# A hybrid RWKV-7 / S5 layer on one core: late tiles two abreast, a gate pair in the other order, stores on another queue, products on another engine, one scan behind the level

## The chip, the cores and the metric

The kernel runs on one core of a Trainium2 chip. The metric is the device time in microseconds of one launch. The engines of the core are named as in the profile: PE is TensorE (matrix products; PEld its weight loads), DVE is VectorE, ACT is ScalarE, POOL is GpSimd and SP is SyncE, which issues most of the DMA transfers. An engine whose name ends in q (SPq, POOLq) is its queue of DMA issues.

## What is computed

One layer over 1024 tokens of width 1024, in fp32:

```python
h = rms_norm(x, norm_mix_pre)
proj = h @ w_in                         # RWKV r, k, v, low-rank downs | S5 input u | two gates
gates = sigmoid(proj[..., -2048:] + b_gate)
o_rwkv = rwkv7_branch(...) @ w_branch_rwkv   # per head: S = S*w + (S a) b' + v k',  y = S r
o_s5 = s5_branch(...) @ w_branch_s5          # complex diagonal scan, then gelu(y) * sigmoid(y @ w_glu + b_glu)
mixed = (g_rwkv * o_rwkv + g_s5 * o_s5) @ w_out
x = x + rms_norm(mixed, norm_mix_post)
h = rms_norm(x, norm_ffn_pre)
z = causal_conv3(h @ w_up); gate, val = split(z)
x = x + rms_norm((gelu(gate) * val) @ w_down, norm_ffn_post)
```

## The kernel before, in words

All activations stand transposed: channels on the 128 partitions, tokens along the free dimension, in two halves of 512 tokens (`th` 0 and 1). A product of fp32 accuracy is made of three matmuls: both operands are split into a high and a low part (weights `wh` on ACT at L157 and `wl` on DVE at L158, from a tile `wf` that SP loads at L156), and `mm3_steps` issues for each of the contraction tiles high by high (L173), low by high (L174) and high by low (L175). One output tile of 128 channels by 512 tokens over eight contraction tiles is therefore 24 matmuls.

PE's instruction order is written out by hand. `drive` steps through generators ("lanes"), each of which names the time until it may go on (constants T_...), in a clock that it advances itself; whenever no lane is due, the next step of a list of background tiles (`fill`) is issued. DVE, ACT, POOL and SP take their order from a scheduler with priorities; each of them then runs strictly in that order.

From 0 to about 255 us the kernel makes the S5 scan and the first projections (`s5_lane`, `tab_lane`, `mix_in`). The projection tiles are stored to memory, all on SP's queue: TZ, TA and TG by `lowrank` (L999), RKV by `rkv` (L1006), and the gates GT by `gate_tiles` (L1035), where ACT writes tanh of the tile at L1034.

From about 255 to 815 us the RWKV branch runs in four pieces i = 0 to 3 (pairs of head groups by token halves), each with two fronts (`rwkv_front`), a matrix inverse (`rwkv_inv`), a `rwkv_level` and a `rwkv_chain` of eight steps; the background is the sixteen gate tiles, two at a time for both halves, then `merge(0)` and the output projection of half 0 with the S5 GLU tiles of half 1 (`out_glu`). A front loads k, TZ, TA and r at L659 and v at L696 (SP), scans TZ (L674, DVE), and makes the products `ar1` and `bk1` on GpSimd (L683 and L684); DVE's L681 and L714 stand beside these. The level begins with two DVE transposes (L787) whose result `ld` PE multiplies at L790. `merge(0)` needs the RWKV output of half 0 (YR, loaded at L1155 on POOL's queue and split at L227/L228) and the S5 output (YU, loaded on POOL's queue at L1119, gelu on ACT, split at L1125/L1126).

From about 815 to 1045 us comes the tail: the S5 part of the merge of half 1 (`merge_s5`), the last `rwkv_out`, its RWKV part (`merge_rk`, results halved and split at L232/L233), the output projection of half 1 (`outproj`), two norms of each half (`mid_norms`) and the first MLP units (`first_units`, whose inputs `h` are split at L227/L228). The rest is the fast up-projection (to about 1400 us) and the down-projection.

## Time and profile before

| | |
|---|---|
| time, median of 3 runs | 1628.59 us (1625.99 to 1630.82) |
| time of the profiled execution | 1626.5 us |
| its span | 1624.7 us |
| mean granted TensorE clock | 0.967 |
| PE busy | 1505.0 us (93%) |
| DVE busy | 1157.2 us (71%) |
| ACT busy | 717.6 us (44%) |
| POOL busy | 175.9 us (11%) |

PE is busy for 93% of the span, and the granted clock is a little under full: a stall of PE shows both as idle time ahead of an instruction, and in the stretches after it in which the clock column is below 1. The idle times are listed by the line that waited and by the instruction that ended the wait. DMA issues are not counted as busy on the queue that issues them.

### The profile page before, as it was taken

Reading aid. Unit: us, or ns where it says so; the run is one execution under the profiler, and the core shown is the slowest. Engines: PE = TensorE matmul, PEld = TensorE weight load, DVE = VectorE, ACT = ScalarE, POOL = GpSimd, SP = SyncE. Lnnn points to the kernel's source line nnn. Section 1 sums busy time; section 2 is a strip of 40 time slices with the busy share of each in tenths; the row PEclk is TensorE's granted clock in tenths of the full one; section 3 lists DMA queues with packets and bytes.
Section 4 is the critical chain, followed back from the end, with each engine's and each line's share of the span. In section 5 each row is a group of like instructions: output and inputs, shape, how many; then the busy total and the mean of one; then the engine's idle time right before and its main releaser. Section 6 shows DMA issues by size and latency. Waiting matters only on the chain. (4 is left out here: it accounts for less than half of the span.)

```text
span 1624.7 us, 23434 instructions
## 1 busy us (share of the span) xinstructions
PE 1505.0 (93%) x8644; PEld 1200.3 (74%) x8644; DVE 1157.2 (71%) x2103; ACT 717.6 (44%) x1173; POOL 175.9 (11%) x251
## 2 busy tenths in 40 slices
PE   5998998999989997899978999999999999999995
PEld 4887887787666774666756878788888888788784
DVE  7888774565534687575478479987777777788777
ACT  5445433232444344446633445544454444443451
POOL 0030003133012133211020000000000000000000
PEclk9999999999998997999988999999999999999997
DMA  5353344343341256535255363322222224862722
GB/s 190 110 158 124 97 130 143 117 130 116 90 145 67 76 179 175 142 106 163 84 187 190 107 193 130 137 71 91 78 78 91 91 79 160 293 227 96 234 85 104
DMA packets 116387, 213.72 MB, mean 132 GB/s; under 512 B 22272, under 2 KB 28416, under 8 KB 116272
## 3 DMA queue, kind: packets, MB, share of 16 engines
q1 hardware_dynamic: 102960, 175.78, 33.8%
q0 software_dynamic: 11152, 32.20, 6.7%
q10 hardware_dynamic: 2160, 4.24, 0.7%
q8 instruction: 68, 1.11, 0.3%
q14 instruction: 47, 0.39, 0.1%
HBM read 157.12 MB, written 52.95 MB: 129 GB/s over the span
## 5 line engine op out<-in xcount | busy, mean ns | idle before, releaser
L173 PE MATMUL gm<-hh,wh 128*128 128x512 f32 x688 | 298.5, 434 | 17.9 <-DVE ev L961 5.5
L174 PE MATMUL gm<-hl,wh 128*128 128x512 f32 x688 | 277.8, 404 | 3.3 <-DVE hl L1126 2.0
L175 PE MATMUL gm<-hh,wl 128*128 128x512 f32 x688 | 276.4, 402 | 0.0
L158 DVE TENSOR_TENSOR wl<-wf,wh 128x512 fp32r<-128x512 f32 x183 | 127.9, 700 | 115.1 <-ACT wh L157 113.4
L157 ACT CAST wh<-wf 128x512 fp32r<-128x512 f32 x183 | 113.3, 620 | 185.2 <-PE gm L174 94.0
L173 PEld LDWEIGHTS gm<-hh,wh 128*128 128x128 f32 x688 | 133.5, 194 | 54.6 <-ACT hh L1125 6.3
L174 PEld LDWEIGHTS gm<-hl,wh 128*128 128x128 f32 x688 | 134.0, 195 | 30.6 <-DVE hl L228 4.3
L175 PEld LDWEIGHTS gm<-hh,wl 128*128 128x128 f32 x688 | 133.6, 194 | 30.2 <-DVE wl L158 0.7
L1608 PE MATMUL d<-xl,wh 128*128 128x512 f32 x308 | 120.3, 391 | 3.1 <-DVE xl L228 3.1
L1607 PE MATMUL d<-xh,wh 128*128 128x512 f32 x308 | 120.2, 390 | 2.0 <-DVE zg L1463 2.0
L1609 PE MATMUL d<-xh,wl 128*128 128x512 f32 x308 | 119.9, 389 | 0.0
L1433 PE MATMUL rp<-t,h 128*128 128x512 f32 x216 | 84.4, 391 | 2.2 <-ACT p L1447 1.6
L1435 PE MATMUL rp<-t,l 128*128 128x512 f32 x216 | 84.2, 390 | 0.5 <-DVE l L228 0.5
L1434 PE MATMUL rp<-t,h 128*128 128x512 f32 x216 | 84.1, 389 | 0.0
L1608 PEld LDWEIGHTS d<-xl,wh 128*128 128x128 f32 x308 | 57.8, 188 | 16.7 <-DVE xl L228 4.8
L1607 PEld LDWEIGHTS d<-xh,wh 128*128 128x128 f32 x308 | 57.8, 188 | 14.4 <-DVE zg L1463 2.4
L1609 PEld LDWEIGHTS d<-xh,wl 128*128 128x128 f32 x308 | 57.8, 188 | 11.9
L227 ACT CAST h<-r 128x1024 fp32r<-128x1024 f32 x34 | 35.8, 1054 | 61.1 <-PE rp L1434 29.6
L228 DVE TENSOR_TENSOR l<-r,h 128x1024 fp32r<-128x1024 f32 x34 | 41.6, 1225 | 29.2 <-ACT h L227 27.7
L1454 DVE SCALAR_TENSOR_TENSOR y<-zv,vecs,y 128x1023 f32<-128x1023 f32 (+1 forms) x36 | 46.1, 1281 | 8.6 <-ACT y L1452 8.6
L1433 PEld LDWEIGHTS rp<-t,h 128*128 128x128 f32 x216 | 40.5, 188 | 11.8 <-ACT p L1447 2.4
L1447 ACT COPY p<-rp 128x512 f32<-128x512 f32 x54 | 31.1, 575 | 37.2 <-PE rp L1435 37.2
(446 smaller groups left out, 3400.4 us busy)
## 6 DMA issues: line engine op xcount, KB each, us to landing
wf<-in_w_in_dram SPq DMA_DIRECT2D x72, 256.0 KB, 3.0
r<-in_w_up_dram SPq DMA_DIRECT2D x36, 512.0 KB, 3.9
st<-in_w_down_dram SPq DMA_DIRECT2D x55, 256.0 KB, 4.3
st<-ACT SPq DMA_DIRECT2D x44, 256.0 KB, 4.7
wf<-in_w_up_dram SPq DMA_DIRECT2D x36, 256.0 KB, 2.9
ACT<-y POOLq DMA_DIRECT2D x18, 512.0 KB, 2.9
GT<-ev SPq DMA_DIRECT2D x32, 256.0 KB, 2.4
wf<-in_w_br_dram SPq DMA_DIRECT2D x32, 256.0 KB, 2.8
```

Of the source, the lines that this page charges most:

```text
L157: nc.scalar.copy(h[:, :n], f[:, :n])
L158: nc.vector.tensor_tensor(l[:, :n], f[:, :n], h[:, :n].bitcast(F32), ALU.subtract)
L173: mm(ps, a, xh[k], start=k == 0, stop=False)
L174: mm(ps, a, xl[k], start=False, stop=False)
L175: mm(ps, b, xh[k], start=False, stop=k == n - 1)
L1433: mm(ps, wh[:, c], xh, start=first and k == 0, stop=False, skip_group_check=True)
L1434: mm(ps, wh[:, c], xl, start=False, stop=False, skip_group_check=True)
L1435: mm(ps, wl[:, c], xh, start=False, stop=k == 3, skip_group_check=True)
L1454: V.scalar_tensor_tensor(y[:, lag:], z[:, 0:1024 - lag], self.vec(nme, i), y[:, lag:], ALU.mult, ALU.add)
L1607: mm(ps, wh[:, c], xh[:, x], start=start, stop=False, skip_group_check=True)
L1608: mm(ps, wh[:, c], xl[:, x], start=False, stop=False, skip_group_check=True)
L1609: mm(ps, wl[:, c], xh[:, x], start=False, stop=stop, skip_group_check=True)
```

## The change

Every one of these is in one version. PE's matmuls are the same in number and shape.

1. `skewed` computes two output tiles abreast: six of the eight contraction tiles for both, then the last two for both. It is used for the first two tiles of `outproj` of half 1 and for the first MLP unit's two tiles (`up1_pair`, there in the order KORD in which `mid_norms` makes the inputs).
2. The stores of TZ, TA, TG, RKV and GT, and the loads of v, are issued by GpSimd's queue instead of SP's.
3. The scan of a front is put, for the scheduler only, behind the transposes of the level before it (`levelled`).
4. The products `ar1` and `bk1` (four for each front, 32 in all) are made on DVE instead of GpSimd.
5. The last gate pair (tiles 14 and 15) does half 1 first; between the halves `merge_values` issues the preparation of the merge's inputs, S5's (`xs0`, through `ev` tiles) included, which `merge` issued after its first gate before. YR is loaded straight into the tile of the low part.
6. The last `rwkv_out` gets the priority HPN and comes due T_LF = 11 after its start instead of T_LN = 16; the S5 GLU tiles of half 1 are issued up to two after each output tile from the fifth on (before: one, from the fourth on), with y loaded ahead of the matmuls; `mid_norms(0)` starts when `merge_rk` has been issued instead of in `merge_s5`, and T_N5 goes from 55 to 24.

The order shows the third and fourth on DVE, at the level of the second piece (i = 1), whose transposes read `gr_3231`; `ld_4601` and `ld_4610` are the TZ tiles of the next piece's two fronts. Before:

```order
L906 TENSOR_TENSOR ld_4584<-ld_4584,ld_4586 128x512
L158 TENSOR_TENSOR wl_4854<-wf_4855,wh_4853 128x512
L906 TENSOR_TENSOR ld_4584<-ld_4584,ld_4588 128x512
L674 SCALAR_TENSOR_TENSOR ld_4601<-csts,ld_4601 128x512
L787 STREAM_TRANSPOSE ld_4632<-gr_3231 32x512 x2
L674 SCALAR_TENSOR_TENSOR ld_4610<-csts,ld_4610 128x512
L681 TENSOR_TENSOR ld_4827<-ld_4827,ld_4599 128x512
L714 SCALAR_TENSOR_TENSOR ld_4605<-ld_4605,vecs,ld_4827 128x512
L681 TENSOR_TENSOR ld_4888<-ld_4888,ld_4608 128x512
L714 SCALAR_TENSOR_TENSOR ld_4614<-ld_4614,vecs,ld_4888 128x512
```

and in the changed kernel:

```order
L929 TENSOR_TENSOR ld_4584<-ld_4584,ld_4588 128x512
L801 STREAM_TRANSPOSE ld_4632<-gr_3231 32x512 x2
L686 SCALAR_TENSOR_TENSOR ld_4601<-csts,ld_4601 128x512
L686 SCALAR_TENSOR_TENSOR ld_4610<-csts,ld_4610 128x512
L695 TENSOR_TENSOR ld_4827<-ld_4827,ld_4599 128x512
L697 TENSOR_TENSOR ar_4593<-ld_4605,gr_4595 64x8x64
L697 TENSOR_TENSOR ar_4593<-ld_4614,gr_4595 64x8x64
L698 TENSOR_TENSOR bk_4594<-ld_4827,ld_4601 64x8x64
L697 TENSOR_TENSOR ar_4593<-ld_4605,gr_4595 64x8x64
L697 TENSOR_TENSOR ar_4593<-ld_4614,gr_4595 64x8x64
L728 SCALAR_TENSOR_TENSOR ld_4605<-ld_4605,vecs,ld_4827 128x512
L698 TENSOR_TENSOR bk_4594<-ld_4827,ld_4601 64x8x64
```

The transposes now stand ahead of both scans, directly behind the last sums of `rwkv_out`, and products of `ar` and `bk` follow the scans on the same engine.

The fifth shows on ACT, around the end of the gate tiles, where `hh` from L1125 (L1148 now) is the high part of an S5 input and L1034 (L1057 now) empties a gate tile. Before:

```order
L1034 ACTIVATE ev_5985<-gm_5960,hb_b_gate 128x512
L227 CAST hh_5928<-ld_5926 128x512
L157 CAST wh_6139<-wf_6141 128x512
L157 CAST wh_6167<-wf_6169 128x512
L757 COPY x_6378<-csts 128x512
L157 CAST wh_6227<-wf_6229 128x512
L1120 ACT_TABLE_LOAD
L1120 ACTIVATE ld_6039<-ld_6039 128x512
L1120 ACTIVATE ld_6046<-ld_6046 128x512
L157 CAST wh_6298<-wf_6300 128x512
L1125 CAST hh_6042<-ld_6039 128x512
L1125 CAST hh_6049<-ld_6046 128x512
```

and in the changed kernel:

```order
L1057 ACTIVATE ev_5905<-gm_5816,hb_b_gate 128x512
L239 CAST hh_5951<-hl_5952 128x512
L157 CAST wh_6014<-wf_6016 128x512
L1143 ACT_TABLE_LOAD
L1143 ACTIVATE ev_5908<-ev_5908 128x512
L157 CAST wh_6065<-wf_6067 128x512
L1148 CAST hh_5911<-ev_5908 128x512
L1143 ACTIVATE ev_5915<-ev_5915 128x512
L701 COPY gr_5702<-rsy_5862 128x512
L157 CAST wh_6088<-wf_6090 128x512
L1148 CAST hh_5918<-ev_5915 128x512
L1143 ACTIVATE ev_5922<-ev_5922 128x512
```

The gelu of the S5 inputs and their high parts stand now between the two halves of the last gate pair (two more gate tiles are emptied behind the last row shown), with the load of the activation table ahead of them; before, they came after the last gate tile and five weight casts.

The first shows on PE at the start of `outproj` of half 1, where `t` are the last four of the eight inputs, in the order in which `merge_rk` finishes them, and `mm` and `ch` the first two output tiles. Before, from the second of these four:

```order
L173 MATMUL mm_8691<-t_1676_8621,wh_8685 128x512
L174 MATMUL mm_8691<-t_1677_8622,wh_8685 128x512
L175 MATMUL mm_8691<-t_1676_8621,wl_8686 128x512
L173 MATMUL mm_8691<-t_1683_8648,wh_8685 128x512
L174 MATMUL mm_8691<-t_1684_8649,wh_8685 128x512
L175 MATMUL mm_8691<-t_1683_8648,wl_8686 128x512
L173 MATMUL mm_8691<-t_1690_8675,wh_8685 128x512
L174 MATMUL mm_8691<-t_1691_8676,wh_8685 128x512
L175 MATMUL mm_8691<-t_1690_8675,wl_8686 128x512
L173 MATMUL ch_8732<-e_8486,wh_8720 128x512
L174 MATMUL ch_8732<-e_8487,wh_8720 128x512
L175 MATMUL ch_8732<-e_8486,wl_8721 128x512
```

and in the changed kernel, from the same input:

```order
L174 MATMUL mm_8630<-t_1654_8548,wh_8612 128x512
L175 MATMUL mm_8630<-t_1655_8549,wh_8612 128x512
L176 MATMUL mm_8630<-t_1654_8548,wl_8613 128x512
L174 MATMUL ch_8631<-e_8413,wh_8618 128x512
L175 MATMUL ch_8631<-e_8414,wh_8618 128x512
L176 MATMUL ch_8631<-e_8413,wl_8619 128x512
L174 MATMUL ch_8631<-e_8440,wh_8618 128x512
L175 MATMUL ch_8631<-e_8441,wh_8618 128x512
L176 MATMUL ch_8631<-e_8440,wl_8619 128x512
L174 MATMUL ch_8631<-e_8467,wh_8618 128x512
L175 MATMUL ch_8631<-e_8468,wh_8618 128x512
L176 MATMUL ch_8631<-e_8467,wl_8619 128x512
```

The third and fourth of them (t_1683 and t_1690 before) followed at once; now the first six inputs of the second tile stand ahead of them.

The diff, without what only passes things on:

```diff
-    def mm3_steps(self, ps, w, wk, xh, xl):
+    def mm3_steps(self, ps, w, wk, xh, xl, ks=None, first=True, last=True):
         wh, wl = w
-        n = len(xh)
-        for k in range(n):
+        ks = list(ks or range(len(xh)))
+        for k in ks:
             j = wk + k
-            self.open += (k == 0) - (k == n - 1)
+            a0, z0 = first and k == ks[0], last and k == ks[-1]
+            self.open += a0 - z0
             mm = self.nc.tensor.matmul
-            mm(ps, a, xh[k], start=k == 0, stop=False)
+            mm(ps, a, xh[k], start=a0, stop=False)
             mm(ps, a, xl[k], start=False, stop=False)
-            mm(ps, b, xh[k], start=False, stop=k == n - 1)
+            mm(ps, b, xh[k], start=False, stop=z0)
+    def skewed(self, tiles, xs, ks, late):
+        xh, xl = [x[0] for x in xs], [x[1] for x in xs]
+        ps = [self.gmp() for _ in tiles]
+        ks = list(ks)
+        for p, (w, _) in zip(ps, tiles):
+            yield from self.mm3_steps(p, w, 0, xh, xl, ks[:-late], last=False)
+        for p, (w, use) in zip(ps, tiles):
+            yield from self.mm3_steps(p, w, 0, xh, xl, ks[-late:], first=False)
+            use(p)
...
-        def ld(src):
+        def ld(src, q=nc.sync):
             t = self.tg("ld", NLD)
-            nc.sync.dma_start(t, src[:, o])
+            q.dma_start(t, src[:, o])
...
-        V.tensor_tensor_scan(tz, self.cst("smask"), tz, 0.0, ALU.mult, ALU.add)
+        scan = V.tensor_tensor_scan(tz, self.cst("smask"), tz, 0.0, ALU.mult, ALU.add)
+        if self.levelled is not None:
+            self.tc.add_manual_dep(scan.ins, self.levelled.ins.name, ORDER)
...
         for h, sl in enumerate(HS):
-            G.tensor_tensor(ar1[h], c64(r)[sl], pe[sl, :, 1:65], ALU.mult)
-            G.tensor_tensor(bk1[h], c64(tk)[sl], c64(tz)[sl], ALU.mult)
+            V.tensor_tensor(ar1[h], c64(r)[sl], pe[sl, :, 1:65], ALU.mult)
+            V.tensor_tensor(bk1[h], c64(tk)[sl], c64(tz)[sl], ALU.mult)
...
             V.scalar_tensor_tensor(bk0[h], c64(kk)[sl], 0.5, c64(tz)[sl], ALU.mult, ALU.mult)
-        v = ld(self.RKV[8 + p])
+        v = ld(self.RKV[8 + p], G)
...
         for h, sl in enumerate(top):
-            V.transpose(xz[sl].rearrange("p u c t -> p (u c) t"), gr[sl, :, :, h, sl].rearrange("p u c t -> p (u c) t"))
+            self.levelled = V.transpose(xz[sl].rearrange("p u c t -> p (u c) t"), gr[sl, :, :, h, sl].rearrange("p u c t -> p (u c) t"))
...
+    def urgent(self, gen):
+        while True:
+            with self.tc.high_priority(HPN - HP2):
+                r = next(gen, None)
+            if r is None:
+                return
+            yield r
...
         V.tensor_tensor(yn, yn, y.unsqueeze(2).to_broadcast([128, 16, 64]), ALU.mult)
-        yield 0, T_LN
+        yield 0, T_LF if final else T_LN
...
         ws = [self.load_w(self.a["w_in"][mt]) for mt, _ in jobs]
-        for th in range(2):
+        for th in (1, 0) if between else (0, 1):
                 use(th, ps)
-            if between and th == 0:
+            if between and th:
...
                         nc.gpsimd.tensor_scalar(t, t, 1.0, 1.0, ALU.add, ALU.mult)
-                    nc.sync.dma_start(dst[p][:, th * 512:th * 512 + 512], t)
+                    nc.gpsimd.dma_start(dst[p][:, th * 512:th * 512 + 512], t)
                 y = self.shifted(ps, mt, th)
-                self.nc.sync.dma_start(self.RKV[mt][:, th * 512:th * 512 + 512], y)
+                self.nc.gpsimd.dma_start(self.RKV[mt][:, th * 512:th * 512 + 512], y)
...
             self.nc.scalar.activation(t, ps, AF.Tanh, bias=self.hb["b_gate"][:, m:m + 1], scale=0.5)
-            self.nc.sync.dma_start(self.GT[m][:, th * 512:th * 512 + 512], t)
+            self.nc.gpsimd.dma_start(self.GT[m][:, th * 512:th * 512 + 512], t)
...
-    def glu_tile(self, m, xs, t, y, to):
+    def glu_tile(self, m, xs, t, y, to, ahead=False):
         w = self.load_w(self.a["w_glu"][m])
+        if ahead:
+            y = lambda v=y(): v
...
+        if not self.xs0:
+            for b in range(4):
+                y = self.s5_y(self.ev((128, 8, 64)), b, 0)
+                self.xs0.append(self.pair(1, 4 + b))
+                self.s5_split(*self.xs0[b], y)
             return
-        self.br0 = []
         for k in range(4):
-            y = self.tg("ld", NLD)
-            self.nc.gpsimd.dma_start(y, self.YR[k][:, 0:512])
-            self.br0.append(self.pair(0, k))
-            self.split(*self.br0[k], y)
+            hh, hl = self.pair(1, k)
+            self.nc.gpsimd.dma_start(hl.bitcast(F32), self.YR[k][:, 0:512])
+            self.br0.append((hh, hl))
+            self.split(hh, hl, hl.bitcast(F32))
...
             self.merge_values()
-        br = self.br0
-        xs = []
-        def inputs():
-            for b in range(4):
-                y = self.s5_y(self.tg("ld", NLD, s8), b, 0)
-                xs.append(self.pair(1, 4 + b))
-                self.s5_split(*xs[b], y)
+        br, xs = self.br0, self.xs0
             if i < NK:
-                first.append(self.hp[1].tile([128, 512], F32, tag=f"h{'lh'[i // 4]}{i % 4}", name=self.nm("hl"), bufs=1))
+                first.append(self.hp[0].tile([128, 512], F32, tag=f"h{'lh'[i // 4]}{i % 4}", name=self.nm("hl"), bufs=1))
                 yield from self.gate(0, i, 0, br[0:4], self.ev(), first[i])
-            if i == 0:
-                inputs()
...
             self.br5[m] = self.slots("eb", m)
-            yield from self.glu_tile(m, xs, self.et(), lambda: self.s5_y(self.et(s8), m, 1), self.br5[m])
+            yield from self.glu_tile(m, xs, self.et(), lambda: self.s5_y(self.et(s8), m, 1), self.br5[m], True)
...
             yield from self.outproj_tile(0, m, mg, self.mx0)
-            if self.glu and m >= 3 and self.now >= self.glu_ready:
-                yield from self.glu.pop(0)
+            for _ in range(2):
+                if self.glu and m >= 4 and self.now >= self.glu_ready:
+                    yield from self.glu.pop(0)
...
             self.split_half(*mg[m], t)
+        self.merged = True
...
-        nc, hp = self.nc, self.hp[th]
         yield from self.mm3_steps(ps, w, 0, [x[0] for x in mg], [x[1] for x in mg])
+        self.outproj_end(th, m, mx, ps)
+    def outproj_end(self, th, m, mx, ps):
+        nc, hp = self.nc, self.hp[th]
...
     def outproj(self, th, mg, mx):
-        for m in range(NK):
+        yield from self.skewed([(self.load_w(self.a["w_out"][m]), lambda ps, m=m: self.outproj_end(th, m, mx, ps))
+                                for m in range(2)], mg, range(NK), 2)
+        for m in range(2, NK):
...
         else:
-            yield 0, lambda: self.y0 is not None
-            yield 0, T_RS
+            yield 0, lambda: self.merged
+            yield 0, T_PN
...
         self.h[th] = [None] * NK
-        for k in (0, 4, 1, 5, 2, 6, 3, 7):
+        for k in KORD:
...
+    def up1_pair(self, i, th):
+        y = []
+        yield from self.skewed([(self.load_w(self.a["w_up"][j]), lambda ps, j=j: y.append(self.conv1(ps, j, th)))
+                                for j in (i, FT + i)], self.h[th], KORD, 2)
+        return y
...
         for i in range(NFIRST):
-            ga = yield from self.up1_steps(i, th)
-            va = yield from self.up1_steps(FT + i, th)
+            if i:
+                ga = yield from self.up1_steps(i, th)
+                va = yield from self.up1_steps(FT + i, th)
+            else:
+                ga, va = yield from self.up1_pair(i, th)
...
         self.mark, self.chained, self.glu, self.glu_ready = False, False, [], 0.0
-        self.opened, self.outs, self.br0, self.y0 = False, 0, None, None
+        self.opened, self.outs, self.br0, self.xs0, self.y0, self.merged, self.levelled = False, 0, [], [], None, False, None
...
             out = self.rwkv_out(d)
-            r = next(out)
-            if i == 3:
-                yield r
-                yield from out
+            if i < 3:
+                r = next(out)
+            else:
+                yield from self.urgent(out)
 NEVA = 4
-T_KN, T_BK, T_GR, T_INV, T_LV, T_CH, T_LN = 17.0, 13.0, 2.5, 62.0, 1.0, 0.8, 16.0
+T_KN, T_BK, T_GR, T_INV, T_LV, T_CH, T_LN, T_LF = 17.0, 13.0, 2.5, 62.0, 1.0, 0.8, 16.0, 11.0
 T_X, T_GLU = 3.0, 25.0
-T_N0, T_RS, T_N1, T_N2, T_N4, T_N5, T_N3 = 2.5, 4.0, 2.2, 5.0, 1.6, 55.0, 2.0
+T_N0, T_RS, T_N1, T_N2, T_N4, T_N5, T_N3 = 2.5, 4.0, 2.2, 5.0, 1.6, 24.0, 2.0
 NET = 5
+T_PN = 8.0
+KORD = (0, 4, 1, 5, 2, 6, 3, 7)
...
 HPW, HPN = 400000, 500000
+ORDER = mybir.DependencyInfo(mybir.DependencyClass.NoSync, mybir.DependencyReason.SCHED_ONLY)
```

## The prediction

> **What bounds the kernel now.** I read the page first, then PE's waits by line, then the windows in which the granted clock is half, and last the timeline around the largest waits.
>
> ```profile
> PE 1505.0 (93%) x8644; PEld 1200.3 (74%) x8644; DVE 1157.2 (71%) x2103; ACT 717.6 (44%) x1173; POOL 175.9 (11%) x251
> PEclk9999999999998997999988999999999999999997
> ```
>
> PE is the bound: of the span of 1624.7 us it is idle for 120, and a few slices between the thirteenth and the twenty-second, and the last, are below full clock. The change leaves PE's matmuls as they are, so all that it can win is idle time and clock. The waits behind the idle time, over the whole trace (line, total in us, times, longest):
>
> ```profile
> PE chb L790 <- DVE ld L787: 10.1, 2, 9.6
> PE mm L173 <- ACT t L232: 5.7, 2, 4.1
> PE gm L173 <- DVE ev L961: 5.5, 1, 5.5
> PE gm L173 <- ACT hh L1125: 5.3, 1, 5.3
> PE rp L704 <- DVE gr L706: 5.3, 3, 3.7
> PE mm L174 <- DVE hl L228: 5.0, 4, 3.4
> PE gm L173 <- ACT hh L227: 4.0, 3, 1.8
> PE gm L173 <- ACT e L232: 3.6, 2, 2.3
> PE mm L173 <- ACT hh L227: 3.4, 3, 1.2
> PE gm L173 <- DVE hl L1146: 2.3, 1, 2.3
> ```
>
> Every row belongs to a place that the change touches. And the stretches at half clock that follow such waits (window; PE busy, PEld, DVE, ACT, POOL; PEclk, DMA share, GB/s):
>
> ```profile
> 280.28:287.11 6.83, 6.22 (x15) 4.86 (x16) 4.27 (x29) 1.75 (x3) 0.00 (x0) 0.50 0.44 154
> 485.08:498.73 13.65, 8.90 (x77) 5.98 (x78) 7.67 (x6) 4.57 (x8) 8.42 (x8) 0.50 0.28 104
> 614.78:621.60 6.82, 6.08 (x18) 4.38 (x17) 5.92 (x14) 2.96 (x5) 3.92 (x7) 0.50 0.78 230
> 631.85:645.50 13.65, 8.70 (x25) 5.61 (x27) 10.08 (x14) 8.93 (x13) 2.65 (x3) 0.50 0.49 118
> 679.64:683.05 3.41, 3.41 (x23) 2.25 (x23) 3.21 (x10) 1.64 (x3) 0.90 (x1) 0.50 0.09 35
> 819.58:826.41 6.83, 5.01 (x11) 3.63 (x12) 5.85 (x19) 2.13 (x4) 1.61 (x3) 0.50 0.44 136
> 850.30:857.13 6.83, 4.11 (x10) 3.15 (x11) 4.42 (x7) 1.26 (x2) 0.54 (x1) 0.50 1.00 371
> 884.44:894.68 10.24, 7.81 (x16) 5.08 (x17) 4.98 (x8) 3.47 (x6) 0.00 (x0) 0.50 0.40 129
> 939.05:945.88 6.83, 6.35 (x19) 5.38 (x20) 3.51 (x15) 0.62 (x1) 0.00 (x0) 0.50 0.23 85
> ```
>
> All are multiples of about 3.41 us. Half of PE's busy time in such a window is lost, since the same work takes half as long at full clock. So a place is worth its idle time plus half of the busy column: about 50 us in the waits' rows and 28 us here (56.6 us busy, halved), 78 us together without the waits that stay small. That is the ceiling.
>
> **The change part by part.** The scan behind the level (place A):
>
> ```profile
> 478.98 0.69 DVE L906 TENSOR_TENSOR ld<-ld,ld 128x512 f32<-128x512 f32 x1
> 479.99 0.38 SPq L911 DMA_DIRECT2D YR<-ld  x1
> 480.47 0.44 SPq L659 DMA_DIRECT2D ld<-TZ  x1
> 487.54 1.23 DVE L674 TENSOR_TENSOR_SCAN ld<-csts,ld 128x512 f32<-128x512 f32 x1 [7.87 <-DMA ld<-TZ]
> 488.68 1.41 DVE L787 STREAM_TRANSPOSE ld<-gr 32x512 f32<-32x512 f32 x2
> 489.41 0.31 PE L790 MATMUL chb<-ld,gr 32*32 32x32 f32 x2 [9.64 <-DVE ld L787]
> YR<-ld SPq DMA_DIRECT2D x6, 256.0 KB, 3.4
> ```
>
> DVE stood 7.87 us on a TZ load that SP issued only at 480.47, and the level's transposes stood behind that scan. Now they stand ahead of it. DVE is free from 479.67 (L906), so they begin at 479.7, or at 483.4 if their `ld` buffer waits for the store of YR issued at 479.99 (3.4 us to landing), and PE goes on 0.7 us after the first. PE's 10.1 us become 1 to 4.5, and of the half-clock loss of 4.5 (8.90/2) none to 1.7 (half a window of 3.41) stays. Gain 8.4 to 13.6; I take 11. What is late next is the scan itself, which still needs its load, and behind it the next front; that front waits for the level anyway, so nothing is charged.
>
> The products on DVE (place B, the front of piece 0 at 270 us):
>
> ```profile
> 270.22 1.82 DVE L714 SCALAR_TENSOR_TENSOR ld<-ld,vecs,ld 128x512 f32<-128x512 f32 x1
> 276.66 1.85 DVE L714 SCALAR_TENSOR_TENSOR ld<-ld,vecs,ld 128x512 f32<-128x512 f32 x1 [2.34 <-POOL ar L683]
> 278.43 1.75 DVE L158 TENSOR_TENSOR wl<-wf,wh 128x512 fp32r<-128x512 f32 x1
> 280.10 0.74 DVE L961 SCALAR_TENSOR_TENSOR ev<-gm,vecs,ev 128x511 f32<-128x511 f32 x1
> L692 DVE SCALAR_TENSOR_TENSOR ar<-gr 64x512 f32<-64x512 f32 x16 | 10.9, 684 | 0.3
> ```
>
> PE waits 5.5 us for the eviction at 280.10. Ahead of it DVE waits 2.34 us for GpSimd, and five operations (three of them shown) run beside GpSimd's products at up to 1.85 us where L961 of the same size takes 0.74 alone: 5 x 1.0 us. Four of the new products, at 0.684 us from L692's row (same shape), now stand ahead of that eviction: 2.7 us. Balance 2.3 + 5.0 - 2.7 = 4.6 us earlier, so the wait falls to about 1 and half of the clock loss of 3.1 (6.22/2) goes: 6. At L704 (3.7 us at 313 us) the same may help by 0 to 4; I take 1. B is 7, from 2 (DVE's own queue decides) to 11. Over the kernel 32 x 0.684 = 22 us are added to DVE, and GpSimd's 32 products go, with what they slowed. Where DVE has no idle time that is a cost: I charge 3 for the fronts after the first, from 0 to 8.
>
> The last gate pair and the merge's inputs (place C, 606 to 650 us):
>
> ```profile
> 606.00:652.00 46.00, 34.46 (x144) 24.32 (x144) 34.06 (x58) 18.30 (x27) 16.13 (x23) 0.78 0.59 166
> 1060.00:1380.00 320.00, 319.00 (x1406) 263.94 (x1407) 244.34 (x269) 155.93 (x186) 8.54 (x16) 1.00 0.27 92
> 630.17 0.62 ACT L157 CAST wh<-wf 128x512 fp32r<-128x512 f32 x1 [4.14 <-DMA wf<-in_w_glu_dram]
> ```
>
> PE is idle for 11.5 of these 46 us, and loses 7.4 more to the clock (half of 6.08 + 8.70): 18.9. (The second row is the steady part of the MLP: 319.00/1406 = 0.227 us a matmul, so a step of three is 0.68 and a tile of eight steps 5.4 us.) ACT's gelu of the S5 inputs begins after a weight cast that waited 4.14 us for its DMA, and so PE waits at L1125; YR's splits (L227) are late in the same way. Two gate tiles of half 0, 11 us of PE, now lie between the loads' issue and their use. Against it: the last gate tiles are emptied behind three gelus on ACT, and one stall of about 3 us there is likely; and DVE, busy 34.06 of 46 us, also has piece 3's front. I take 13, from 4 to 19. The wait at L1146 (2.3 us at 677, where a gate load stood late on SP) and the half clock behind it (1.7), with other short waits up to 712 us: 3, from 0 to 9 (place D).
>
> The tail. At 814 to 858 us (place E) PE's waits on `e` (L232) and on `hl` and `hh` (L228, L227) add up to 10, the half-clock windows at 819 and 850 to 4.6. GLU tiles now come at least one output tile ahead of the S5 merge, and behind the last `rwkv_out` stand sixteen steps of `merge_s5` instead of nine: 7 x 0.68 = 4.8 us more cover for the splits, longer than the longest wait there (3.4). The price is that `rwkv_out` comes seven steps nearer to the chain's end; its DVE work has priority now. 10, from 4 to 14.5. `outproj` (place F): the waits on `t` (5.7 in two) hit steps seven and eight of the first tile; abreast, step seven comes six steps or 4.1 us later, which just covers the longest (4.1). 5.7 + 7.81/2 = 9.6 at most; I take 8, from 5. First MLP unit (place G): waits of at most 1.2 us each, 3.8 in all, and 3.2 of clock (6.35/2). In KORD the sixth input is needed at the sixth step but one is made only every 1.4 us (a product of 0.74 and a split of 0.69 on DVE, by the rows above), so a part stays: 3, from 0 to 7. The later norm of half 0 is covered by `outproj`'s eight tiles of 5.4 us.
>
> The stores on GpSimd's queue:
>
> ```profile
> SPq L1035 <- ACT ev L1034: 130.8, 24, 16.9
> bv<-ld POOLq DMA_DIRECT2D x8, 256.0 KB, 3.6
> GT<-ev SPq DMA_DIRECT2D x32, 256.0 KB, 2.4
> 625.99 4.62 POOL L775 DMA_DIRECT2D gr<-xd  x8 [3.80 <-DMA xd<-x]
> ```
>
> SP no longer stands up to 16.9 us on a gate tile with weights and loads queued behind. That gain is in B to D. The waits move to GpSimd, where the inverse's transfers (L775 and those before it) and the loads of YR and YU queue behind them. A store's landing of 3.6 instead of 2.4 us is hidden, since it is read hundreds of us later. I charge 3, from nothing to 15.
>
> By the Trainium skill (SBUF — State Buffer, "SBUF: two separate sides") descriptors of a transfer issued by GpSimd can't be written while DVE holds the shared port in a two-port operation; its example goes from 620 to 3100 ns. The rows above show 1.2 us between the queues, not 2.5; by the page's figure the 80 stores would land 2.5 us later each, an estimate, and the sum would be the same as long as no one waits for them.
>
> The sum: -11 (A) -7 (B) -13 (C) -3 (D) -10 (E) -8 (F) -3 (G) = -55, +3 for DVE, +3 for the queue. These gains are taken one by one, though PE that arrives earlier meets ACT, DVE and loads that have not become faster; I give a tenth of the span's remaining slack back, 6 us or half of D and E. Together -43. On the profiled 1626.5 us that is 1583.5; the median of the runs is 2.1 higher, so I predict 1585.6 for it.
>
> **The rivals.** *DVE and ACT take over between 590 and 860 us.* In 606 to 652 DVE is busy for 74% with PE waiting; if its order there decides, C and E keep only 4 each, D and G nothing, F 5, and the sum is -11 -7 -4 -4 -5 +3 +3 = -25: 1604. For it speaks DVE's share; against it that PE waits there for ACT splits behind DMAs.
>
> *GpSimd's queue holds the inverse* (slower). A GT store whose tile is late stands ahead of `xd` or `gr<-xd`; by SP's row a store waits up to 16.9 us. The transfer of piece 2 is issued from 625.99 to 630.61 and its level's transposes follow at 638.2, so a wait beyond some 8 us makes PE idle: 16.9 - 8 = 9 us and half of that for the clock, 13 us a level. With three levels hit, 39 us, and C lost besides (13), the kernel is at -43 + 52 = +9: 1638. Two such waits leave it just below the time before, so it decides from the third on. Against it: PE makes the gate tiles in the same order in which the queue stores them, so such a store is late only when PE is.
>
> *Everything goes*: with each term near its upper end, 12 + 10 + 17 + 6 + 13 + 9 + 6 - 5 = 68, the time is 1560.
>
> *The scan's edge does nothing*, since the scheduler could have put it so elsewhere: then A stays and the time is 1597. The order on DVE speaks against it.
>
> By the Trainium skill (TensorE: Matmul & The Clock Gate, "What's actually happening") the clock halves after an idle window of about 3.4 us. Here the stretch at 939.05 follows waits of at most 1.2 us each, so several short waits do as well, and I leave clock loss where waits stay. By the page's rule B and D would win some 3 us more, 1582.
>
> **How the numbers follow.** Forecast 0.55 (1568 to 1600 is its own range), DVE and ACT 0.20, the scan's edge alone 0.05, all of it 0.07, the queue 0.13. The range from 1560 to 1620 holds the first three and leaves out the queue's case and half of the fourth, some 0.17. Within 0.3% (4.9 us, about what a measurement of this kernel can tell from no change) of before lies only a mild form of the queue's case, with one or two levels hit: 0.04. Slower by more: 0.09. Faster: 0.87.
>
> **What would show it.** A: the transposes (L801 of the changed kernel) at once behind the last sum of `rwkv_out`, PE's wait on them under 3 us, no half clock at 485. B: no wait of PE on a DVE eviction near 275 us, and L728 at 0.74 us. C: PE's wait on the S5 splits under 2 us. E to G: waits on `t`, `e`, `hl` under 1 us each. The prediction is wrong if PE's waits move to `gr` of the fronts (L706 before) or to transfers on GpSimd's queue, or if the kernel's mean clock stays below 0.98.

## The result: 23 us faster where 43 were forecast

The changed kernel took 1604.96 us (median of four runs, 1595.80 to 1608.95) beside 1628.30 for the kernel before; the ratio is 0.9848 with a 95% interval of 0.9802 to 0.9895. Six more runs of it, later, gave 1600.49 (ratio 0.9824, 0.9795 to 0.9854). Below, "the changed kernel" stands for about 1601, the median of the ten. The forecast was 1585.6: the direction is right, the size half of it. The time lies inside the forecast's range (1560 to 1620), next to its first rival (1604). One of the twelve executions of the run with the edge alone took 2134.78 us at a granted clock of 0.652; it is left out of that run's ratio.

Its profiled execution was the slowest of the four, 1608.95 us with a span of 1607.2. The page after:

```profile
PE 1503.5 (94%) x8644; PEld 1204.1 (75%) x8644; DVE 1153.9 (72%) x2135; ACT 716.8 (45%) x1173; POOL 180.1 (11%) x307
PEclk9999999999997998999999999999999999999997
```

PE's idle time fell from 120 to 104 us, and the thirteenth slice (the second level) is lower on the clock than before. PE's waits by line (line, total in us, times, longest), those that bear on the change; the longest of all, 11.5 us at the start of the kernel, was 11.9 before:

```profile
PE mm L174 <- DVE t L1402: 5.0, 1, 5.0
PE gm L174 <- DVE hl L1171: 4.8, 1, 4.8
PE rp L718 <- DVE gr L720: 4.1, 3, 3.0
PE rp L924 <- DVE yn L918: 3.0, 1, 3.0
PE gm L174 <- ACT ev L1057: 2.9, 1, 2.9
PE rp L718 <- DVE bk L698: 2.7, 1, 2.7
PE gm L174 <- DVE last L986: 2.2, 1, 2.2
PE chb L804 <- DVE ld L801: 2.0, 2, 1.5
```

The waits of before on the transposes (10.1), on `t` (5.7) and on the S5 splits (5.3) are gone or small. The first, second, fourth, fifth and sixth rows are new, or at least twice as long as their forerunner.

To see where time was won and lost, I took the start of the same PE instruction in the two traces of the changed kernel and in that of before. The table gives how much shorter each stretch became.

| stretch of PE's order | place | forecast | first profile | second profile |
|---|---|---|---|---|
| start to the first chain (413 us before) | B | 7 | 1.0 | 6.0 |
| to the fronts' products of piece 2 (543) | A | 11 | 1.2 | 4.1 |
| to the third level (656) | C, with 3 for DVE | 10 | 11.1 | 11.2 |
| to the fourth chain (767) | D | 3 | -7.3 | -5.7 |
| to the first `t` of `outproj` (879) | E | 10 | 11.2 | 11.5 |
| to its last (932) | F | 8 | 8.1 | 8.1 |
| to the fast up-projection's `t` (1050) | G | 3 | -5.8 | -9.0 |
| to the end | none | 0 | -2.1 | 0.1 |
| sum | | 43 (with 9 given back) | 17.5 | 26.2 |

Eight small matmuls of a norm, 0.8 us, moved from the fifth stretch to the sixth; the other stretches hold the same number of matmuls in both kernels. C, E and F came as forecast, within 2 us. A, D and G did not, and these three are the missing 20 us and more.

### The profile page after: what moved, and what is told of

Read it like the earlier page. It is cut to its first block, busy times and chain, and to the rows that moved or that the text cites. A ratio compares the mean times of both kernels' runs of the same rounds, so it can differ in the third digit from the quotient of the medians.

```text
span 1607.2 us, 23412 instructions
## 1 busy us (share of the span) xinstructions
PE 1503.5 (94%) x8644; PEld 1204.1 (75%) x8644; DVE 1153.9 (72%) x2135; ACT 716.8 (45%) x1173; POOL 180.1 (11%) x307
## 5 line engine op out<-in xcount | busy, mean ns | idle before, releaser
L1422 POOL DMA_DIRECT2D ACT<-y x18 | 9.6, 535 | 341.2 <-DVE y L1421 341.2
```

## The experiments

Two theories stood at the start. The waits theory: the missing time went into new waits that the new orders made, at places that can be named. The clock theory: the waits fell as forecast, and half-clock stretches came back by chance.

### The changed kernel again

No edit.

> The changed kernel once more, unchanged. Two theories of why it gained 23 us of the forecast 43. The waits theory: new waits took the rest (5.0 us of PE at 940 us behind the first MLP unit's evictions, 4.8 at 664 behind a gate load, 3.0 at 821 behind yn), so they stand in this profile too, at the same lines and within 1 us of the same length, and the times stay near 1605. The clock theory: the stretches at half clock (52 us lost in the first profile, 55 before the change) fall by chance on short waits, so the waits are the same here but the half-clock stretches are not, and the times spread over more than 8 us and go with the mean clock.

Measured: 1600.49 us. The waits at 664, 821 and 940 us of the first profile stand in this one too, at 4.86, 3.04 and 4.98 us. The half-clock stretches shift: by the prediction's measure (half of PE's busy time in them) 35.5 us were lost instead of 39.6; before the change it was 37.9. Within the six runs the two ends are 1604.48 us at a mean clock of 0.969 and 1595.83 at 0.977. So both theories hold a part: the waits are fixed, and the clock spreads the times of one kernel over 9 us.

### The scan's edge alone

```diff
 (kernel before)
+        scan = V.tensor_tensor_scan(tz, ...)
+        if self.levelled is not None:
+            self.tc.add_manual_dep(scan.ins, self.levelled.ins.name, ORDER)
... (and `self.levelled = V.transpose(...)` in the level)
```

> The kernel before with the scan's edge behind the level alone. The prediction's step (place A): 8.4 to 13.6 us faster, 1617. The rival from the first profile after, that the level only starts earlier and then waits on ACT and runs at half clock (there A was 12 us ahead at 486 us and 2.4 ahead at 513): 1 to 4 us faster, 1624 to 1627.

Measured: 1631.59 us, ratio 1.0014 (0.9996 to 1.0032). The edge alone gains nothing, where the prediction's step gave 8.4 to 13.6 and the rival 1 to 4. PE's waits from 476 to 515 us, and then ACT and GpSimd there:

```profile
PE chk L794 <- ACT gr L795: 6.0, 1, 6.0
PE chb L792 <- DVE ld L789: 1.7, 2, 1.2
```

```profile
499.38 0.81 ACT L682 ACTIVATE ld<-ld,ka,ka_h 128x512 f32<-128x512 f32 x1 [5.08 <-POOL bk L686]
500.80 0.72 ACT L795 COPY gr<-chk 32x256 f32<-32x256 f32 x2
```

```profile
498.08 1.26 POOL L686 TENSOR_TENSOR bk<-ld,ld 64x512 f32<-64x512 f32 x1
```

The level starts on time (the wait on the transposes is 1.2 us), and stalls at its second step: the copy it needs (L795) stands on ACT behind an operation of the next front (L682), which needs a buffer that GpSimd's product `bk` still reads. In the kernel before, the same front ran before the level.

### The first MLP unit's evictions first

```diff
 (changed kernel; in `up1_pair`, the lambda of the two skewed tiles)
+    def first_conv(self, y, ps, j, th):
+        with self.tc.high_priority(HPN):
+            y.append(self.conv1(ps, j, th))
-        lambda ps, j=j: y.append(self.conv1(ps, j, th))
+        lambda ps, j=j: self.first_conv(y, ps, j, th)
```

> The changed kernel with the evictions (the causal convolution) of the first MLP unit's two skewed tiles put ahead of the norm of half 1 on DVE and ACT. The waits theory: PE's wait of 5.0 us at 940 us goes, and the half-clock loss of about 3 behind it, so 5 to 8 us faster than the changed kernel, 1598. The rival, that DVE is the bound there and the wait moves to the norm of half 1 (its inputs then come late for the first units of half 1): within 2 us of the changed kernel.

Measured: 1588.65 us, ratio 0.9752 (0.972 to 0.9784), 12 us faster than the changed kernel beside it, 4 more than expected. In the changed kernel DVE did this before the wait ended (935 to 945 us):

```profile
935.58 0.74 DVE L1302 SCALAR_TENSOR_TENSOR mx<-mx,vecs,rp 128x512 f32<-128x512 f32 x1
936.24 0.15 DVE L1399 COPY edge<-mm 128x2 f32<-128x2 f32 x1
940.61 0.74 DVE L1402 SCALAR_TENSOR_TENSOR t<-mm,vecs,t 128x511 f32<-128x511 f32 x1
943.78 1.39 DVE L1402 SCALAR_TENSOR_TENSOR t<-mm,vecs,t 128x510 f32<-128x510 f32 x2
```

L1302 is the norm of half 1, whose eight steps run from 920.75. The two skewed tiles end at about 922.8 and 924.2, after that norm has started, and on DVE their convolutions (from 936.24) stand behind all of it. DVE then stands 2.03 us more on ACT for the next unit's second tile, and PE's fifth tile, which waits for the first one's bank in PSUM, starts at 944.7. With the evictions first, the waits of PE from 905 to 960 us are these:

```profile
PE ch L174 <- DVE t L1402: 1.3, 1, 1.3
PE rp L258 <- ACT tm L270: 1.2, 1, 1.2
```

From the end of `outproj` to 1050 us this kernel is 1.3 us shorter than the kernel before, where the changed kernel was 5.8 and 9.0 longer. So 7 to 10 of the 12 us are gained at this place. The rest may be clock: 25.0 us are lost to half clock in this profile, against 39.6 and 35.5, and only 1.9 and 6.3 us of these differences lie at this place.

### The first MLP unit's tiles apart

```diff
 (changed kernel)
-            if i:
+            if True:
                 ga = yield from self.up1_steps(i, th)
```

> The changed kernel with the first MLP unit's two tiles one after the other again, contraction in the natural order. If the skew of this unit is what made the wait at 940 us (both tiles end together, behind the norm of half 1), that wait falls below 1 us and the waits at 909 us come back to about 3.8, with about 3 of clock: 0 to 4 us faster than the changed kernel. If the skew is not its cause, the wait stays and the time is 4 to 7 us slower.

Measured: 1594.60 us, ratio 0.9789 (0.9761 to 0.9817): 6 us faster than the changed kernel, 2 beyond the range. PE's waits from 890 to 960 us:

```profile
PE mm L174 <- ACT hh L239: 2.6, 2, 2.4
PE mm L175 <- DVE hl L240: 1.1, 2, 0.7
```

The wait of 5.0 is gone and those on the splits are back, 3.7 together. So it is the skew itself that made the wait at 940 us, by ending both tiles late. From the end of `outproj` to 1050 us this kernel is still 2.3 us longer than the kernel before, so the skew with its evictions first is worth 3.6 us there, by one profile of each.

### The changed kernel without the edge

```diff
 (changed kernel)
-        if self.levelled is not None:
-            self.tc.add_manual_dep(scan.ins, self.levelled.ins.name, ORDER)
```

> The changed kernel without the scan's edge behind the level. By the prediction's step A the edge is worth 8.4 to 13.6 us: 1610 or more. By what the edge alone gave (nothing: PE's wait moved from the transposes to the level's second step, behind the front on ACT) and by the five profiles in which the second level runs some 17 us at half clock whatever wait stands ahead of it, it is worth 1 to 4 us even beside the products on DVE: 1602 to 1605.

Measured: 1608.72 us, ratio 0.9877 (0.9852 to 0.9902), about 7 us slower than the changed kernel, between the two expectations. PE waits on the transposes again (470 to 500 us):

```profile
PE chb L802 <- DVE ld L799: 9.8, 2, 9.4
```

Beside the products on DVE the edge is worth something.

### The products back on GpSimd

```diff
 (changed kernel)
-            V.tensor_tensor(ar1[h], ...)
-            V.tensor_tensor(bk1[h], ...)
+            G.tensor_tensor(ar1[h], ...)
+            G.tensor_tensor(bk1[h], ...)
```

> The changed kernel with the 32 products ar1 and bk1 back on GpSimd. If the edge and the products need each other (the scan behind the level makes the front late, and ACT's copies of the level stand behind a front operation that waits for GpSimd's bk), the wait of 6 us in the second level comes back as in the run of the edge alone, with the 5.5 us at 270: 10 to 16 us slower than the changed kernel, 1611 to 1617. If they are independent, only B's price comes back (4 to 7 us): 1605 to 1608.

Measured: 1612.10 us, ratio 0.9894 (0.9873 to 0.9915), 11 us slower than the changed kernel. PE's waits from 470 to 500 us, from 595 to 645 us, and from 262 to 320 us:

```profile
PE chk L806 <- ACT gr L807: 5.8, 1, 5.8
PE gm L174 <- ACT ev L1057: 9.2, 1, 9.2
PE gm L174 <- DVE ev L984: 1.8, 1, 1.8
```

The wait in the second level is back as in the run of the edge alone. And PE's wait for the eviction of a gate tile at 605 us, 2.9 us in the changed kernel, is 9.2. But the 5.5 us near 275, which the expectation counted on, did not come back: the same matmul waits 1.8 (third row), with 1.2 more at an earlier tile. The size is inside the expected range, its parts are not the expected ones.

### The edge and the products together on the kernel before

```diff
 (kernel before, with the edge)
+            V.tensor_tensor(ar1[h], ...)
+            V.tensor_tensor(bk1[h], ...)
```

(in place of GpSimd's two lines)

> The kernel before with the scan's edge and the products on VectorE, nothing else. The edge alone gave nothing (1632 beside 1628), and in the changed kernel taking away the edge costs some 7 us and taking away the products some 11. If the two need each other, the pair gives 8 to 13 us here: 1615 to 1620. If they are independent, and the edge is worth nothing, the pair gives what the products give at 270 us, 3 to 7: 1621 to 1625.

Measured: 1617.12 us, ratio 0.9934 (0.991 to 0.9957), 10.6 us faster than before; the edge alone was no faster. The stretch of place A (first chain to the fronts of piece 2) gains 6.3 us here and loses 1.0 with the edge alone; that of place B gains 8.5 and nothing. So on A the two need each other; the products without the edge were not run on the kernel before. In the second level (PE's waits from 465 to 500 us, and the window at half clock: PE, PEld, DVE, ACT, POOL, PEclk, DMA share, GB/s):

```profile
PE chb L792 <- DVE ld L789: 1.7, 2, 1.2
PE chk L794 <- ACT gr L795: 1.2, 1, 1.2
```

```profile
473.37:483.61 10.24, 10.24 (x79) 7.06 (x78) 4.89 (x7) 4.41 (x8) 1.09 (x2) 0.50 0.64 203
```

No wait there is longer than 1.2 us, PE is recorded as busy for the whole window, and it still runs at half clock, 10.24 us long, losing 5.1. In the kernel before, the same level lost 4.5 at half clock after a wait of 9.6. So taking the long wait away did not win the clock part of step A.

### The stores back on SP's queue

```diff
 (changed kernel)
-  nc.gpsimd.dma_start(...)   # TZ, TA, TG, RKV, GT
+  nc.sync.dma_start(...)
-        v = ld(self.RKV[8 + p], G)
+        v = ld(self.RKV[8 + p])
```

> The changed kernel with the 80 stores and the loads of v back on SP's queue. By the prediction, SP's waits on gate tiles come back (130 us in 24 before) and part of C with them: 4 to 12 us slower, 1605 to 1613. The rival, that SP's waits lie beside PE's work and the queue makes no difference: within 2 us.

Measured: 1598.81 us, ratio 0.9818 (0.9796 to 0.9841), the same as the changed kernel or 2 us faster. SP's waits suggest why the move gains nothing. Before:

```profile
SPq L156 <- DVE wl L158: 337.5, 117, 9.4
```

In the changed kernel:

```profile
SPq L156 <- DVE wl L158: 454.2, 119, 18.9
```

With the stores back on SP:

```profile
SPq L156 <- DVE wl L158: 304.7, 113, 13.1
SPq L1058 <- ACT ev L1057: 119.1, 24, 10.8
```

The waits on gate tiles left SP, and as much more is spent on weight buffers. And in the stretch to the third level the gain is not smaller (11.7 us). What moved is the wait at 664 us (D). SP in the changed kernel, and with the stores back:

```profile
644.90 19.97 SPq L156 DMA_DIRECT2D wf<-in_w_br_dram  x5
664.92 0.43 SPq L1168 DMA_DIRECT2D ev<-GT  x1
```

```profile
642.47 9.30 SPq L156 DMA_DIRECT2D wf<-in_w_br_dram  x3
651.82 0.71 SPq L1168 DMA_DIRECT2D ev<-GT  x1
```

Five weight loads, each waiting for its buffer, stand ahead of the gate load in the changed kernel, three here. PE's wait is 4.8 us there and 2.3 here, and the stretch of place D loses 3.4 us instead of 7.3 and 5.7.

### The gate loads on GpSimd's queue, with the evictions first

```diff
 (changed kernel with the evictions first)
-        (nc.gpsimd if th else nc.sync).dma_start(t, self.GT[8 * j + m]...)
+        nc.gpsimd.dma_start(t, self.GT[8 * j + m]...)
```

> The first MLP unit's evictions first (as in the run that gave 1589), and the gate loads of the merge of half 0 on GpSimd's queue too. The waits theory: PE's 4.8 us at 657 us end with a gate load that SP issued at 664.9 behind five weight loads; off that queue the wait goes and with it 2 to 3 us of half clock: 5 to 8 us faster than those 1589, 1581 to 1584. The rival: these loads wait for buffers and hold GpSimd's transfers of the inverse, so the third or fourth level comes late: 1590 or more.

Measured: 1592.87 us, ratio 0.9771 (0.9741 to 0.98), 4 us more than without this edit (1588.65), within the spread of both. PE's wait there, then GpSimd's queue, DVE and ACT:

```profile
PE gm L174 <- ACT ev L1160: 5.5, 1, 5.5
```

```profile
649.40 0.58 POOL L1168 DMA_DIRECT2D ev<-GT  x1
663.73 0.89 POOL L1142 DMA_DIRECT2D ev<-YU  x1 [13.75 <-DVE x L779]
664.92 0.56 POOL L1168 DMA_DIRECT2D ev<-GT  x1 [0.29 <-DVE x L779]
```

```profile
661.64 1.02 DVE L1161 SCALAR_TENSOR_TENSOR ev<-ev,ev 128x512 f32<-128x512 f32 x1
662.69 0.69 ACT L1160 ACTIVATE ev<-gm,hb_b_glu 128x512 f32<-128x512 f32 x1 [2.67 <-DVE ev L1161]
```

PE waits from 657.96 to 663.43, so the gate load issued at 664.92 can't have ended that wait, and the one before it was issued 8 us ahead of it. The wait now ends with ACT's emptying of an S5 GLU tile (L1160), which waits for DVE's multiplication of the GLU tile before (L1161). So the gate load was not the only thing late there: with it out of the way the next one decides, and the wait stays. That GLU path was not tried.

### The merge's inputs back

```diff
 (changed kernel: inproj, merge_values and merge as before)
-        for th in (1, 0) if between else (0, 1):
+        for th in range(2):
-            if between and th:
+            if between and th == 0:
```

> The changed kernel with the last gate pair in the order 0, 1 again and the merge's inputs (YR and S5's) prepared where they were before. The prediction's step C was 13 us, from 4 to 19; in the five profiles of the changed order PE gains 11 to 12 us between the third front and the third level. So 9 to 13 us slower than the changed kernel: 1610 to 1614. The rival, that this gain comes from the stores and loads on other queues: within 4 us.

Measured: 1609.53 us, ratio 0.989 (0.9865 to 0.9914), 8 us slower than the changed kernel, one less than expected. PE's waits from 596 to 650 us:

```profile
PE gm L175 <- DVE hl L1149: 5.0, 3, 2.9
PE gm L174 <- ACT hh L239: 4.9, 3, 3.0
PE gm L174 <- ACT hh L1148: 1.6, 1, 1.6
```

The waits on both splits are back. From the fronts of piece 2 to the third level this kernel gains 1.2 us on the kernel before, the changed one 11: step C is shown, and it is the gate pair's order with the early inputs that makes it.

### Evictions first, stores on SP

> The first MLP unit's evictions first, and the stores and loads of v back on SP's queue. Putting the stores back gave 1599 beside 1601, and the evictions first 1589. If they add up: 1584 to 1588. If GpSimd's queue helps once the tail is shorter: above 1590.

The edits are the two shown. Measured: 1589.33 us, ratio 0.977 (0.9747 to 0.9793), as fast as with the evictions alone (1588.65) and between the two expectations. The queue of the stores makes no difference with the shorter tail either; they do not add up.

### And `yn` later

```diff
 (as the run before)
-T_LF = 11.0
+T_LF = 13.5
```

> As the run before, with the transposes of the last rwkv_out due at 13.5 instead of 11 after its start (three steps, some 2 us of PE's work, later). The wait on yn (3.0 us in every profile, at 812 us, and a half-clock stretch of 3.41 behind it) falls to about 1: 2 to 4 us faster than the run before. The rival: the splits behind rwkv_out lose that cover, and PE waits for hh or hl instead: no faster.

Measured: 1594.32 us, ratio 0.9792 (0.9767 to 0.9817): no faster, and by the medians 5 slower. PE's waits from 800 to 845 us:

```profile
PE ch L175 <- DVE hl L240: 2.9, 1, 2.9
PE mm L174 <- DVE e L1171: 1.1, 1, 1.1
PE rp L924 <- DVE yn L918: 1.0, 1, 1.0
```

The wait on `yn` fell from 3.0 to 1.0 us and 2.9 us turn up at the splits behind it, which did not wait in the run before, as the rival said: `rwkv_out` is one dependency chain, and steps put ahead of its transposes are missing behind them.

The best version that was run is the changed kernel with the evictions first: 1588.65 us, 2.5% faster than the kernel before.

## Why the prediction was half right

*Step B* (products on DVE): the mechanism held on the kernel before. L728 runs at 0.743 to 0.752 us where L714 took 1.42 on average. With edge and products alone the wait of 5.5 us at 280 us is gone, and with the edge alone it stays (5.8). In the changed kernel it is gone too, and PE waits 2.2 us (1.3 in the second profile) at an earlier eviction. But there the products are not the only cause: with them back on GpSimd the wait is 1.8 and the stretch to the first chain still gains 4.7 us, and which other part of the change does that is not shown. The stretch gave 1.0 and 6.0 in the two profiles, 8.5 with edge and products alone. 7 lies among them, and the clock decides how much shows: the half-clock loss up to the first chain was 8.2 us before, 11.6 in the first profile and 5.0 in the second. The 3.0 us on `gr` (L720) at 310 us stayed, within the 0 to 4 given.

*Step A* failed, as a term of the sum: 11 became 1.2 and 4.1, and 6.3 with edge and products alone. The wait on the transposes did fall from 10.1 to 2.0, as worked out. Two things were wrong. "Nothing is charged" for the next front was one: the front's operations now lie inside the level, on ACT, and cost PE up to 4.0 us there with the products on DVE and 6 with GpSimd, so without the products the edge was worth nothing. The clock was the other: of 4.5 us I let none to 1.7 stay, and the level lost 4.7 in its own window in the first profile (490.66 to 500.90) and 5.1 in the second, with 3.4 in a later one (504.31 to 511.14 in the first). A window of 10.24 us stands at this level in every profile with the edge and the products, though no wait there is over 4.0 us, and in some none over 1.8. I had taken half clock as the price of the long wait ahead of it.

*Step C* held: 11 us with DVE's charge, in both profiles, and the undone version lost 8. The stall of about 3 us on ACT's eviction came (2.9), and so did DVE's charge of 3: the fronts' products wait 2.7 and 0.9 us for DVE's `bk` at 626 us.

*Step D* failed. The 3 us were to come from SP's freed queue; instead PE's wait behind a gate load rose from 2.3 to 4.8, since the scheduler put two more weight loads ahead of that load. I took "SP no longer stands up to 16.9 us on a gate tile" for a gain without looking for what SP waits on next. That wait is 2.5 of the 9 to 10 us that D is off. In all, PE's waits in this stretch are 4 to 5 us longer than before, and the half-clock loss 3.1 and 1.6 us larger (in the first profile a window of 6.83 us in the fourth level). Why the short waits of the chain and of the fourth level grew is not shown.

*Steps E and F* held, at 11.2 to 11.5 and 8.1 us. The price named in E (`rwkv_out` nearer to the chain's end) was real: the wait on `yn`, 3.0 us.

*Step G* failed with the wrong sign: 3 forecast, 5.8 and 9.0 lost. The waits on the splits fell from 3.8 to 1.7, as said. But the skew's other side was not costed: two tiles abreast end together, so the first is emptied six steps later than before. For `outproj` nothing stood in the way of that eviction. For the MLP unit the norm of half 1 did. The run with the evictions first shows the price: 7 to 10 us in this stretch, 12 by the medians. With that price gone, the skew gains 3.6 us over the tiles apart, about the 3 that were forecast for it.

The clock as a whole was mis-sized in the sum. The mean clock went from 0.967 to 0.968 and 0.971 in the two profiles, and no execution of the changed kernel came above 0.977; the prediction had named a mean below 0.98 as a sign that it is wrong. Some 10 us of half-clock loss went in the stretches of C, E and F in the first profile, and 12 came back elsewhere: at the start, in the second and the fourth level. What the change won is idle time, 119.7 us before, 103.7 and 99.4 after.

The 6 us given back "though PE that arrives earlier meets ACT, DVE and loads" were the right thought with the wrong size, and no place. Of the rivals, the first gave nearly the measured time (1604) for another reason, by luck: C and E, which it cut, came whole. The queue's case did not happen: the stores' move cost some 2 us by the medians, and the stores of GT landed after 3.2 us instead of 2.4, those of RKV after 2.9 instead of 3.2. The longer landing by the Trainium skill's example (SBUF — State Buffer, "SBUF: two separate sides") is not seen here, at most 0.8 us instead of 2.5.

## What to carry to other kernels

An edge that moves a stage ahead on one engine has to be followed through every other in-order engine that both stages use; here it was worth nothing until a second change took away what the other engine then waited for. Two tiles abreast hide late inputs, but both outputs come late and at once: look at what the evicting engine does at that moment, and give their evictions a priority if something long stands there. A wait that leaves a queue is a gain only if the next wait on that queue is shorter: read what it waits for next. And the instruction that ended a wait is only the last that was late: with the gate load out of the way another tile decided, and the wait was as long.

## What was unexpected of the hardware

The granted clock fell to half in a stretch without long waits. In the second level, where 32 by 32 matmuls stand between those of the background tiles, PE was recorded as busy for 10.24 of 10.24 us (79 matmuls) at 0.50 in the run of the edge and the products together. In the 3.41 us ahead of that window PE had been idle for 1.69 us, its longest wait 1.2; in the second profile of the changed kernel a half-clock window followed 3.41 us with 1.06 us idle. The Trainium skill (TensorE: Matmul & The Clock Gate, "What's actually happening") ties half clock to idle windows of about 3.4 us; the windows' length agrees with multiples of 3.41 here, but a whole idle window is not what went ahead of them. Why the clock stayed at half for three such windows of recorded busy time is not shown.

The half-clock stretches also go with the spread of the times. Six runs of the version with the evictions first go from 1580.29 us at a mean clock of 0.982 to 1593.82 at 0.973, so a difference of under 5 us between two of these kernels needs several runs, and one profile can stand 8 us or more from another of the same kernel.
